# Stick-breaking attention by summation by parts: value differences made at the projection, no weights formed

## The chip, the cores and the metric

One core of one Trainium2 chip runs the whole program. The metric is device time in microseconds (us) of one execution; before, it is 3059.33 us, the median of three runs (3055.2 to 3061.43).

Engines by the profile's names: PE (TensorE matmul) with PEld (its weight loads), DVE (VectorE), ACT (ScalarE), POOL (GpSimd), and SP, whose queue issues all DMAs here. L12 is line 12 of the kernel before.

## What is computed

Two layers run in a row on x of 1024 tokens by 1024 features. Each projects x with `w_in`, runs three token mixers on groups of heads (stick-breaking attention and MLA attention with 4 heads each, RWKV-7 with 8), joins them with `w_o`, normalizes, and ends in a gated FFN with a short convolution. Only the stick-breaking mixer changes:

```python
def stick_breaking_attention(q, k, v):
    ...
        z = jnp.einsum('bhqd,bhkd->bhqk', qb, k).astype(jnp.float32) * scale
        past = kpos[None, :] < qpos[:, None]
        log_keep = jnp.where(past, jax.nn.log_sigmoid(-z), 0.0)
        log_later = lax.cumsum(log_keep, axis=3, reverse=True) - log_keep
        w = jnp.where(past, jnp.exp(jax.nn.log_sigmoid(z) + log_later), 0.0)
        return jnp.einsum('bhqk,bhkd->bhqd', w.astype(v.dtype), v)
```

With keep = sigmoid(-z) and K(j) the product of keep over the positions j and later (1 where masked), the weight is w(j) = K(j+1) - K(j). So the sum of w(j) v(j) is also the sum of K(j) (v(j-1) - v(j)), plus an end term.

## The kernel before

**Phase A** (`phase_a`) works with the transposed activations xTh and xTl in SBUF. Each matrix of weights of 128 columns is loaded and split in a high and a low part (`wload`, L200, L201). Its product with x takes 48 matmuls of 128x512 into the PSUM tile `psmm`, in two halves of 24 (`proj_h`, L205 to L207), and ACT copies each half to a tile `pst` (L253). There are 4 buffers of `pst`, and 3 of `psmm` of one half each.

After the RWKV projections come two recurrent chains of 8 steps (`rw_chain(0)` and `rw_chain(1)`, 4 heads each). Chain 1 needs the result of `rw_inv`, a triangular inverse in small steps on DVE (L725 to L767) and PE (L759, L776, L788), which goes out to DRAM (`psd`, L792) and comes back with each step (`PSl`, L831). A step of a chain is L844 (PE), copies to `QC` (DVE L845, L846, ACT L847), L863 (PE) and L866 (DVE) twice, L871 (PE), and its output `rw_chain_y1`/`y2` (L880 to L906).

`proj_sb` (L263) makes the stick-breaking projections beside this. Its function `step` takes one step of chain 1, whatever number it is given. Before, the order is queries and keys of head pair 0, then of pair 1 (one chain step after each), then the values of both pairs, transposed on PE (L281) and copied on DVE (L282), with one chain step after each pair.

**Attention** follows: MLA (`mla`) and stick-breaking (`stick`) blocks of 128 queries take turns. A stick-breaking block (`stick_block`, `stick_post`) is: scores (PE, L388, L389), tanh (ACT, L390), the mask of the diagonal block (POOL, L396), keep from tanh (DVE, L397), the product scan from the right (DVE, L399), the weight from keep and product (DVE, L400), transposes (PE, L339) with copies to SBUF (ACT, L340), and weights times values (PE, L323) with a scaled copy (ACT, L418). Before, keep and the product sit in one of three tiles that POOL clears first (L1194); they lie in the SBUF of the tiles `LA`, `T` and `pd` of `rw_inv`.

The order on each engine is fixed when the program is built: a scheduler with priorities (`PRIORITY`) and costs of its own sorts the instructions of each engine, and an engine takes them in that order. PSUM and SBUF buffers of one tag go round in the order in which the code asks for them. The transposes of values use the PSUM tags `pa`, `py` and `pq`, which the chains use too.

## Time and profile before

| | |
|---|---|
| median of three runs | 3059.33 us |
| profiled execution, its own time | 3062.54 us |
| its span, first to last instruction | 3060.8 us |
| granted TensorE clock, mean | 0.980 of full speed |
| busy: PE, DVE, ACT, POOL | 96%, 58%, 34%, 8% |

The busy shares are means over stages with different limits. PE is pipelined and the ends of its matmuls are modelled, so a PE at 100% is not at its peak. A row of the windows view gives, for one stretch, the busy us of each engine with its number of instructions, the granted clock, the share of DMA time and the GB/s. Matmuls on plain fp32 data appear as two or more records each.

### The profile page before, as it was taken

The page shows a single profiled execution, that of the slowest core. Times are in us where ns is not written, and L with a number is a line of the kernel's source. Part 1 is how long each engine was busy: PE and PEld are TensorE (multiplying, and loading weights), DVE is VectorE, ACT ScalarE, POOL GpSimd, SP SyncE. Part 2 cuts the span into 40 slices and gives each one's busy share as a digit, 9 for nine tenths or more (in the row PEclk, how much of TensorE's full clock was granted, in tenths as well). Part 3 has the DMA queues.
Part 4 walks back from the last instruction along what each step waited for, and adds up shares of the span by engine and source line. Part 5 has one row for each costly group of instructions (what it writes and reads, how often), then busy time and mean ns, then how long its engine had stood idle before and what let it go on. Part 6 is the DMA issues. An engine that isn't in the chain of part 4 may idle for free.

```text
span 3060.8 us, 41867 instructions
## 1 busy us (share of the span) xinstructions
PE 2941.1 (96%) x16572; PEld 2342.6 (77%) x16572; DVE 1774.8 (58%) x2881; ACT 1045.0 (34%) x1801; POOL 234.2 (8%) x308
## 2 busy tenths in 40 slices
PE   8999999989999999999999999999899999999998
PEld 6766777766888888888877677776678888888887
DVE  4579764886644444444645787658865444444436
ACT  5454443763221112121244543447622111212120
POOL 0001121131000000000000011210300000000000
PEclk9999999899999999999999999999999999999999
DMA  4353656324421111111124446563244111111111
GB/s 132 94 153 107 196 178 202 104 59 138 166 62 56 42 42 49 55 49 56 59 80 112 133 121 202 168 206 93 82 134 165 55 42 42 48 55 49 55 49 55
DMA packets 338259, 301.78 MB, mean 99 GB/s; under 512 B 24200, under 2 KB 302992, under 8 KB 338064
## 3 DMA queue, kind: packets, MB, share of 16 engines
q1 hardware_dynamic: 338064, 299.11, 32.3%
q8 instruction: 131, 2.15, 0.3%
q14 instruction: 64, 0.52, 0.1%
HBM read 208.87 MB, written 90.18 MB: 98 GB/s over the span
## 4 chain that ended last, share of the span: by engine, by line
PE 74%; DVE 11%; issue 8%; ACT 3%; DMA 2%; POOL 1%; SPq 0%; POOLq 0%; DVEq 0%; ACTq 0%
PE psmm L205 16%; PE psmm L206 16%; PE psmm L207 16%; PE psps L205 5%; PE psps L206 5%; PE psps L207 5%; PE pspa L844 1%; DVE pd L729 1%; DVE LA L725 1%; PE pspi L788 1%; PE psmt L216 1%; DVE Aa L767 1%; DVE T L730 1%; PE pspa L684 0%; PE pspy L871 0%
## 5 line engine op out<-in xcount | busy, mean ns | idle before, releaser
L206 PE MATMUL psmm<-xTl,whi 128*128 128x512 f32 x2144 | 851.0, 397 | 0.0
L205 PE MATMUL psmm<-xTh,whi 128*128 128x512 f32 x2144 | 850.4, 397 | 0.0
L207 PE MATMUL psmm<-xTh,wlo 128*128 128x512 f32 x2144 | 848.0, 396 | 0.0
L200 ACT CAST whi<-raw 128x1024 fp32r<-128x1024 f32 x152 | 160.3, 1055 | 1059.5 <-PE psmm L206 1043.0
L205 PEld LDWEIGHTS psmm<-xTh,whi 128*128 128x128 f32 x2144 | 405.1, 189 | 89.0 <-issue 5.4
L207 PEld LDWEIGHTS psmm<-xTh,wlo 128*128 128x128 f32 x2144 | 405.3, 189 | 87.9 <-issue 4.2
L206 PEld LDWEIGHTS psmm<-xTl,whi 128*128 128x128 f32 x2144 | 405.3, 189 | 87.9 <-issue 4.4
L201 DVE TENSOR_TENSOR wlo<-raw,whi 128x1024 fp32r<-128x1024 f32 x152 | 185.5, 1220 | 465.3 <-ACT whi L200 447.9
L1056 DVE TENSOR_TENSOR y<-y,psps 128x512 f32<-128x512 f32 x288 | 196.3, 686 | 171.4 <-PE psps L207 171.3
L205 PE MATMUL psps<-wdh,hh 128*128 128x512 f32 x672 | 266.8, 397 | 0.0
L206 PE MATMUL psps<-wdl,hh 128*128 128x512 f32 x672 | 262.9, 391 | 0.0
L207 PE MATMUL psps<-wdh,hl 128*128 128x512 f32 x672 | 259.7, 391 | 0.0
L205 PEld LDWEIGHTS psps<-wdh,hh 128*128 128x128 f32 x672 | 126.1, 188 | 36.8 <-ACT hh L200 6.0
L919 POOL TENSOR_TENSOR lsm<-lsm,small 128x1 f32<-128x1 f32 x32 | 29.0, 905 | 1634.0 <-DVE lsm L918 1634.0
L207 PEld LDWEIGHTS psps<-wdh,hl 128*128 128x128 f32 x672 | 126.2, 188 | 26.9
L206 PEld LDWEIGHTS psps<-wdl,hh 128*128 128x128 f32 x672 | 126.2, 188 | 25.3
L1031 DVE TENSOR_TENSOR cv<-cv,psmm 128x1024 f32<-128x1024 f32 x44 | 53.7, 1221 | 136.1 <-PE psmm L207 131.1
L201 DVE TENSOR_TENSOR wdl<-raw,wdh 128x1024 fp32r<-128x1024 f32 x42 | 51.5, 1225 | 88.6 <-ACT wdh L200 88.6
L1026 ACT ACTIVATE cv<-cv 128x1024 f32<-128x1024 f32 x44 | 46.8, 1063 | 116.0 <-DVE cv L1025 116.0
L844 PE MATMUL pspa<-RBl,PSl 128*128 128x128 f32 x512 | 73.6, 291 | 11.9 <-ACT QC L847 8.9
L844 PEld LDWEIGHTS pspa<-RBl,PSl 128*128 128x128 f32 x512 | 66.5, 200 | 19.5 <-ACT QC L847 10.8
L206 PE MATMUL psmm<-wol,whi 128*128 128x512 f32 x192 | 76.9, 401 | 2.0 <-DVE wol L201 2.0
(442 smaller groups left out, 4568.2 us busy)
## 6 DMA issues: line engine op xcount, KB each, us to landing
raw<-in_ffn_w_up_dram SPq DMA_DIRECT2D x88, 512.0 KB
raw<-in_w_in_dram SPq DMA_DIRECT2D x44, 512.0 KB
raw<-in_ffn_w_down_dram SPq DMA_DIRECT2D x44, 512.0 KB
rbd<-RB SPq DMA_DIRECT2D x64, 256.0 KB
PSl<-psd SPq DMA_DIRECT2D x32, 512.0 KB
RBl<-rbd SPq DMA_DIRECT2D x32, 512.0 KB
psd<-Vz SPq DMA_DIRECT2D x64, 128.0 KB
xxd<-X SPq DMA_DIRECT2D x64, 128.0 KB
```

The lines of the kernel that those rows point to most:

```text
L200: self.nc.scalar.copy(hi, src)
L201: (eng or self.nc.vector).tensor_tensor(lo, src, hi.bitcast(F32), op=ALU.subtract)
L205: mm(out, lh, rh, start=start, stop=False)
L206: mm(out, lh, rl, start=False, stop=False)
L207: mm(out, ll, rh, start=False, stop=stop)
L216: nc.tensor.transpose(pt[:, k * P : k * P + P], xt[:, kk * P : kk * P + P], self.ident)
L725: nc.vector.transpose(LA[r], Af[r, :, q // 2, x0 : x0 + 32].rearrange("p f t -> p t f"))
L729: mul = lambda o, x, y: nc.vector.tensor_tensor(o, x, y, op=ALU.mult)
L844: nc.tensor.matmul(pQ[:, f, e, :], PSh[:, f, h, e, :], RBh[:, f, h, e, :], start=True, stop=True)
L1026: nc.scalar.activation(cv, cv, AF.Gelu)
L1031: nc.vector.tensor_tensor(cv, cv, pg, op=ALU.mult)
L1056: nc.vector.tensor_tensor(y[:, i, hs], y[:, i, hs], ps, op=ALU.add)
```

## The change

1. `proj_sb` projects the values first. From the projected values `d` it makes differences `e` on DVE (e[t] = d[t-1] - d[t], e[0] = -d[0]), transposes and stores them in `svd[0]`; then it replaces the last column of each block of 128 by d[t-1] (the end term), transposes again and stores that in `svd[1]`. So each pair of heads now has two sets of transposes, copies and stores, and one chain step after each set.
2. Queries and keys follow, with one chain step after each, as before. All 8 steps of chain 1 are now asked for inside `proj_sb`; before it was 6.
3. `stick_post` forms keep in place, scans in place, and transposes the scan's result. The weight (L400) is gone, and so are the three cleared tiles.
4. `attn_out` takes the end-term values for the last block and the plain differences for the others. The scale of 0.5 in `av_store` becomes a plain copy.
5. The difference values are loaded into the tiles `LA` and `T` (pair 0), and `pd` and a new tile `mdd` (pair 1).

```diff
     def proj_sb(self, l, pool, step):
         nc, W = self.nc, self.a["w_in"][l]
         for j in range(2):
+            hi, lo = self.wload(W, [(SBV + j * P, P)])
+            d = self.t(pool, [P, S], "pst", bufs=4)
+            self.proj_copy(hi, lo, d)
+            e = self.t(pool, [P, S], "pst", bufs=4)
+            nc.vector.tensor_tensor(e[:, 1:S], d[:, 0 : S - 1], d[:, 1:S], op=ALU.subtract)
+            nc.vector.tensor_scalar(e[:, 0:1], d[:, 0:1], -1.0, None, op0=ALU.mult)
+            self.store_v(e, self.svd[0, j], pool)
+            step(2)
+            nc.vector.tensor_copy(e[:, P - 1 : S : P], d[:, P - 2 : S : P])
+            self.store_v(e, self.svd[1, j], pool)
+            step(2)
+        for j in range(2):
             for base, dst in ((SBQ, self.sqd), (SBK, self.skd)):
...
                 step(4)
-        for j in range(2):
-            hi, lo = self.wload(W, [(SBV + j * P, P)])
...
-            nc.sync.dma_start(self.svd[j], o.rearrange("p (i v) -> p i v", v=P))
+
+    def store_v(self, e, dst, pool):
+        nc = self.nc
+        o = self.t(pool, [P, S], "pst", bufs=4)
+        for q in range(2):
+            pt = self.ps2()
+            for i in range(4):
+                ii = 4 * q + i
+                nc.tensor.transpose(pt[:, i * P : i * P + P], e[:, ii * P : ii * P + P], self.ident)
+            nc.vector.tensor_copy(o[:, q * 512 : q * 512 + 512], pt)
+        nc.sync.dma_start(dst, o.rearrange("p (i v) -> p i v", v=P))
...
-                ms.append(self.nc.tensor.matmul(av[hc], V[:, j, hc], wts[hp][:, j, :], start=j == 0, stop=j == nb - 1))
+                ms.append(self.nc.tensor.matmul(av[hc], (Vd if j == nb - 1 else V)[:, j, hc], wts[hp][:, j, :], start=j == 0, stop=j == nb - 1))
...
+    def stick_steps(self, wp, pr):
+        r3 = lambda t: t.rearrange("p (j v) -> p j v", v=P)
+        if pr:
+            V = r3(self.t(self.ip, [P, S], "pd")), self.t(wp, [P, NT, P], "mdd", bufs=1)
+        else:
+            V = tuple(r3(self.t(self.ip, [P, S], n)) for n in ("LA", "T"))
+        for u in range(2):
+            self.nc.sync.dma_start(V[u], self.svd[u, pr])
+        return V
...
-        nc.vector.tensor_scalar(kp[:, : LL - 1], be[:, 1:LL], -0.5, 0.5, op0=ALU.mult, op1=ALU.add)
-        kv = kp[:, : LL - 1][:, ::-1]
-        nc.vector.tensor_tensor_scan(kv, kv, self.ones.to_broadcast([P, LL - 1]), 1.0, op0=ALU.mult, op1=ALU.mult)
-        nc.vector.scalar_tensor_tensor(be[:, :LL], be[:, :LL], 1.0, kp[:, :LL], op0=ALU.add, op1=ALU.mult)
+        nc.vector.tensor_scalar(be[:, :LL], be[:, :LL], -0.5, 0.5, op0=ALU.mult, op1=ALU.add)
+        kv = be[:, :LL][:, ::-1]
+        nc.vector.tensor_tensor_scan(kv, kv, self.ones.to_broadcast([P, LL]), 1.0, op0=ALU.mult, op1=ALU.mult)
...
-        nc.scalar.mul(ot, av, sc)
+        nc.scalar.copy(ot, av)
```

The scheduler sorts anew, and three places move. In the rows below the lines of the changed kernel are its own: its L292 and L293 are the transposes and copies of `store_v`, L294 its store, L370 the load of difference values; L792, L804, L805 and L808 are L776, L788, L789 and L792 of before, and L847, L850, L860, L863, L879 and L896 are L831, L834, L844, L847, L863 and L880 of before. L205 to L207 and L253 are the same lines in both.

**PE, first layer, at the start of chain 1.** Before, this stands there (`psmm` is a projection, `pspa<-RBl,PSl` the first work of a chain step):

```order
L206 MATMUL psmm_4538<-xTl_133,whi_4506 128x512
L207 MATMUL psmm_4538<-xTh_132,wlo_4507 128x512
L205 MATMUL psmm_4538<-xTh_132,whi_4506 128x512
L844 MATMUL pspa_4067<-RBl_4058,PSl_4059 128x128 x4
L844 MATMUL pspa_4075<-RBl_4058,PSl_4059 128x128 x4
L206 MATMUL psmm_4538<-xTl_133,whi_4506 128x512
L207 MATMUL psmm_4538<-xTh_132,wlo_4507 128x512
L205 MATMUL psmm_4538<-xTh_132,whi_4506 128x512
L844 MATMUL pspa_4113<-RBl_4104,PSl_4105 128x128 x4
L844 MATMUL pspa_4121<-RBl_4104,PSl_4105 128x128 x4
L863 MATMUL pspy_4083<-S_514_3175,QC_4066 64x64 x4
```

Now it is this, from the last work of `rw_inv` on (`pspi<-T`), `pspa<-ident,pst` being a transpose of values:

```order
L804 MATMUL pspi_3898<-LA_3896,Aa_878 128x128 x4
L804 MATMUL pspi_3904<-LA_3896,Aa_878 128x128 x4
L804 MATMUL pspi_3956<-T_3954,Aa_878 128x128 x4
L804 MATMUL pspi_3962<-T_3954,Aa_878 128x128 x4
L860 MATMUL pspa_4083<-RBl_4074,PSl_4075 128x128 x4
L860 MATMUL pspa_4091<-RBl_4074,PSl_4075 128x128 x4
L860 MATMUL pspa_4129<-RBl_4120,PSl_4121 128x128 x4
L879 MATMUL pspy_4099<-S_514_3175,QC_4082 64x64
L860 MATMUL pspa_4137<-RBl_4120,PSl_4121 128x128 x4
L879 MATMUL pspy_4099<-S_514_3175,QC_4082 64x64 x3
L292 MATMUL pspa_4161<-ident_65,pst_4055 128x128 x4
```

Before, 112 projection matmuls of `proj_sb` stand between the first L759 of the second `rw_inv` and the first L844 of chain 1, and 59 behind that. Now 0 stand there and 168 behind, the first of them 56 rows after the chain's start. In the second layer it was 112 and 59 too, and is now 48 and 120, the first one 88 rows after the chain's start. Behind the last projection the chain work of before (16 and 24 matmuls of L863 in the two layers) is gone.

**ACT, first layer, the same place.** Before (`LA<-pspi` and `T<-pspi` end `rw_inv`, `QC` is a chain step, `pst<-psmm` releases a projection):

```order
L789 COPY LA_3896<-pspi_3898 128x512
L789 COPY LA_3896<-pspi_3904 128x512
L789 COPY T_3954<-pspi_3956 128x512
L789 COPY T_3954<-pspi_3962 128x512
L200 CAST whi_4646<-raw_4645 128x1024
L253 COPY pst_4384<-psmm_4411 128x512
L253 COPY pst_4511<-psmm_4512 128x512
L847 COPY QC_4066<-pspa_4067 64x2x256
L847 COPY QC_4066<-pspa_4075 64x2x256
L847 COPY QC_4112<-pspa_4113 64x2x256
L847 COPY QC_4112<-pspa_4121 64x2x256
L253 COPY pst_4511<-psmm_4538 128x512
```

Now:

```order
L805 COPY T_3954<-pspi_3956 128x512
L805 COPY T_3954<-pspi_3962 128x512
L863 COPY QC_4082<-pspa_4083 64x2x256
L863 COPY QC_4082<-pspa_4091 64x2x256
L863 COPY QC_4128<-pspa_4129 64x2x256
L863 COPY QC_4128<-pspa_4137 64x2x256
L896 COPY ys_4147<-pspy_4099 128x256
L897 ACTIVATE yq_4145<-ys_4147 128x256
L863 COPY QC_4197<-pspa_4198 64x2x256
L863 COPY QC_4197<-pspa_4206 64x2x256
L253 COPY pst_4228<-psmm_4229 128x512
L253 COPY pst_4228<-psmm_4255 128x512
```

The two copies at the end are those of the second pair's values. They are what frees `psmm` for the next projections, and they now stand behind the first two steps of chain 1 (three pairs of `QC`) and the first step's output.

**SP, first layer, in chain 1.** Before, the store of values stands behind the loads of a chain step, and its load comes in the attention phase:

```order
L831 DMA PSl_4807<-psd_122 128x1024
L832 DMA RBl_4806<-rbd_120 128x1024
L833 DMA arl_4808<-ard_123 128x256
L284 DMA svd_117<-pst_4564 128x1024
L530 DMA mv_4939<-mvd_116 128x1024
L533 DMA pst_4941<-mqd_114 96x1024
```

Now (`svd<-pst` is a store of value differences, `LA`, `T` and `pd<-svd` load them):

```order
L849 DMA arl_4403<-ard_123 128x256
L294 DMA svd_117<-pst_4154 128x1024
L370 DMA T_5203<-svd_117 128x1024
L847 DMA PSl_4529<-psd_122 128x1024
L848 DMA RBl_4528<-rbd_120 128x1024
L849 DMA arl_4530<-ard_123 128x256
L294 DMA svd_117<-pst_4284 128x1024
L294 DMA svd_117<-pst_4366 128x1024
L370 DMA pd_6317<-svd_117 128x1024
L850 DMA bvl_4404<-bvd_124 128x256
```

The loads of `T` and `pd` now stand one and two rows behind stores that they read from, in front of `PSl` loads of chain 1.

## Rows read from the trace of the kernel before

**Rows 1.** The page's parts 1 and 4: busy time, and the chain that ended last.

```profile
PE 2941.1 (96%) x16572; PEld 2342.6 (77%) x16572; DVE 1774.8 (58%) x2881; ACT 1045.0 (34%) x1801; POOL 234.2 (8%) x308
...
PE 74%; DVE 11%; issue 8%; ACT 3%; DMA 2%; POOL 1%; SPq 0%; POOLq 0%; DVEq 0%; ACTq 0%
```

**Rows 2.** Windows of the first layer: rw_inv's end, chain 1, after the projections, attention.

```profile
core 0: us, PE busy (x) PEld busy (x) DVE busy (x) ACT busy (x) POOL busy (x), PEclk, DMA share, GB/s
414.20:475.70 61.50, 58.17 (x589) 48.20 (x588) 24.91 (x47) 23.89 (x46) 15.35 (x16) 0.94 0.56 164
475.70:518.70 43.00, 42.92 (x367) 33.88 (x368) 22.75 (x67) 14.53 (x30) 7.02 (x8) 1.00 0.58 193
518.70:545.00 26.30, 21.33 (x167) 17.86 (x166) 19.31 (x52) 16.23 (x35) 5.50 (x7) 0.87 0.67 185
545.00:722.00 177.00, 154.95 (x1144) 116.44 (x1143) 150.37 (x292) 119.19 (x302) 37.04 (x50) 0.93 0.31 91
```

**Rows 3.** Windows of the second layer, the same four stretches.

```profile
1939.60:2000.30 60.70, 58.29 (x589) 48.17 (x588) 24.88 (x47) 23.90 (x46) 15.33 (x16) 0.94 0.56 164
2000.30:2038.90 38.60, 38.59 (x338) 32.00 (x339) 20.86 (x61) 13.77 (x29) 6.69 (x7) 1.00 0.65 222
2038.90:2066.50 27.60, 22.75 (x203) 18.84 (x201) 20.96 (x58) 17.02 (x38) 6.14 (x8) 0.94 0.66 184
2066.50:2242.00 175.50, 152.48 (x1142) 114.17 (x1141) 149.42 (x291) 118.51 (x300) 35.94 (x50) 0.95 0.31 92
```

**Rows 4.** Windows of L400 alone, in the attention stretches of both layers.

```profile
core 0: us, DVE busy (x), PEclk, DMA share, GB/s
545.00:722.00 177.00, 25.07 (x32) 0.93 0.31 91
2066.50:2242.00 175.50, 25.15 (x32) 0.95 0.31 92
```

**Rows 5.** Windows inside the first layer's attention, and one of chain steps without projections.

```profile
520.00:535.00 15.00, 10.91 (x102) 8.83 (x100) 11.43 (x26) 9.88 (x17) 1.96 (x3) 1.00 0.88 253
555.00:575.00 20.00, 17.36 (x89) 12.88 (x89) 15.01 (x40) 11.56 (x33) 2.64 (x5) 0.66 0.46 138
585.00:595.00 10.00, 10.00 (x85) 7.74 (x84) 9.81 (x23) 9.40 (x24) 0.13 (x2) 1.00 0.12 32
580.00:620.00 40.00, 37.22 (x325) 29.65 (x325) 38.57 (x81) 32.23 (x85) 2.17 (x5) 1.00 0.26 67
```

**Rows 6.** Waits of PE in the first layer's attention (us in total, times, longest).

```profile
PE psav L339 <- DVE mexp L580: 5.0, 5, 2.7
PE psmm L205 <- ACT whi L200: 3.2, 1, 3.2
PE pspa L339 <- DVE mst L566: 2.6, 2, 2.4
...
PE pspa L339 <- DVE mexp L400: 1.9, 4, 0.8
```

**Rows 7.** Timeline of PE, second layer: a run of 39 projection matmuls, its ends.

```profile
1991.23 0.40 PE L206 MATMUL psmm<-xTl,whi 128*128 128x512 f32 x1
...
1999.89 0.39 PE L205 MATMUL psmm<-xTh,whi 128*128 128x512 f32 x1
```

**Rows 8.** The chain of waits, first layer, from rw_inv's last matmul to chain 1.

```profile
464.74 0.97 PE pspi L788 x8
...
465.73 0.60 ACT T L789
...
466.97 3.99 DMA psd<-T
...
471.03 4.71 DMA PSl<-psd
...
475.78 1.27 PE pspa L844 x9
```

**Rows 9.** Timeline of PE, first layer: four transposes of values and what follows.

```profile
500.61 0.66 PE L281 MATMUL pspa<-ident,pst 128*128 128x128 f32 x4
501.20 0.33 PE L863 MATMUL pspy<-S,QC 128*64 128x64 f32 x2
```

**Rows 10.** DVE groups: a copy of transposed values; an elementwise operation of 128x1024.

```profile
L282 DVE COPY pst<-pspa 128x512 f32<-128x512 f32 x2 | 1.4, 690 | 0.0
...
L201 DVE TENSOR_TENSOR wlo<-raw,whi 128x1024 fp32r<-128x1024 f32 x152 | 185.5, 1220 | 465.3 <-ACT whi L200 447.9
```

**Rows 11.** Timeline of PE, first layer: the same eight records at two clocks.

```profile
442.83 1.78 PE L788 MATMUL pspi<-LA,Aa 128*128 128x128 f32 x8
...
445.64 1.06 PE L788 MATMUL pspi<-LA,Aa 128*128 128x128 f32 x8
```

More of the change, by code (lines that the diff above doesn't have):

```diff
@@ L76, in __init__ @@
         self.sq = 0
-        self.sn = self.kn = 0
+        self.sn = 0
         self.pairs = {}
@@ L271, in proj_sb @@
                 step(4)
-        for j in range(2):
-            hi, lo = self.wload(W, [(SBV + j * P, P)])
-            d = self.t(pool, [P, S], "pst", bufs=4)
-            self.proj_copy(hi, lo, d)
-            o = self.t(pool, [P, S], "pst", bufs=4)
-            for q in range(2):
-                pt = self.ps2()
-                for i in range(4):
-                    ii = 4 * q + i
-                    nc.tensor.transpose(pt[:, i * P : i * P + P], d[:, ii * P : ii * P + P], self.ident)
-                nc.vector.tensor_copy(o[:, q * 512 : q * 512 + 512], pt)
-            step(4)
-            nc.sync.dma_start(self.svd[j], o.rearrange("p (i v) -> p i v", v=P))
+    def store_v(self, e, dst, pool):
[8 more added lines that the diff above has]
+        nc.sync.dma_start(dst, o.rearrange("p (i v) -> p i v", v=P))
     def proj_mla(self, l, pool):
@@ L390, in stick_block, with stick_post @@
             nc.scalar.activation(be[:, a0:a1], s, AF.Tanh, scale=0.0625)
[L391 to L393 removed]
+        self.stick_post(be, i, LL, nb, n, V, hp, pr, wp)
+    def stick_post(self, be, i, LL, nb, n, V, hp, pr, wp):
         nc = self.nc
@@ L584, in mla_post @@
         wt = self.w_transpose(self.wt4[:, self.sn % 6], e, nb)
-        self.pair(("m", pr, i), wt, hp, nb, V, self.mixd[2 + pr], i, wp, "av", 1.0)
+        self.pair(("m", pr, i), wt, hp, nb, V, V, self.mixd[2 + pr], i, wp, "av")
     def q2(self, tp):
@@ L1191, in run @@
                 self.wt4 = self.t(self.ip, [P, 6, NT, P], "Aa")
-                self.kp3 = [self.t(self.ip, [P, S], n) for n in ("LA", "T", "pd")]
-                for t in self.kp3:
-                    nc.gpsimd.memset(t, 0.0)
                 for t in range(MLA_AHEAD):
```

17 lines of the change are left out of this document (6 added, 11 removed).

## Prediction

> **What bounds the kernel now.** I read the page first. PE is busy for 96% of the span, and the chain that ended last is PE for 74% and DVE for 11% [rows 1]. So an operation taken off DVE is worth something only where PE waits for DVE, and an instruction added to PE costs its whole time where PE has no gap. The windows show where that is. Each layer has four stretches that the change touches [rows 2, 3]: the end of `rw_inv` (PE busy 58.17 of 61.5 us in the first layer, 58.29 of 60.7 in the second), chain 1 with projections beside it (42.92 of 43.0 and 38.59 of 38.6: no gap), the rest of chain 1 without projections (21.33 of 26.3 and 22.75 of 27.6), and attention (154.95 of 177.0 and 152.48 of 175.5). PE idles for 22.0 and 23.0 us in attention, and for 5.0 and 4.85 us behind the last projection. It idles little in the other two stretches because projection matmuls lie between the small steps of `rw_inv` and of chain 1. The change lowers the work of DVE in attention, and it moves these projections.
>
> **The work removed.** L400 was 32 instructions per layer, 25.07 and 25.15 us of DVE [rows 4], in stretches where DVE is busy for 150.37 and 149.42 us [rows 2, 3]. The memsets of three tiles were on POOL, which is 8% busy [rows 1], and cost nothing. A copy with a scale and a plain copy are the same pass of ACT over the same tile: nothing.
>
> How much of the 25 us comes back? PE cannot gain more than it idles, 22 us, except by the clock: in 555 to 575 the granted clock is 0.66 (a mix of the levels 2.4 and 1.2 GHz) [rows 5], and fewer waits for DVE may keep it up there. By rows, 20 us at 0.66 lose 20 x 0.34 = 6.8 us. The upper bound is then 22 + 7 = 29 us per layer. The lower bound is 0: in 580 to 620, where DVE is fullest (38.57 of 40 us), PE is busy for 37.22 us already, and in 585 to 595 both are full (10.00 and 9.81 of 10) [rows 5]. The waits of PE that name DVE are also partly of other kinds: MLA's copies and maxima (L566, L580) stand above those for L400 [rows 6], and the former remain. They do come sooner when DVE has a sixth less to do (25 of 150). I take two thirds of the idle time, 15 us, and 2 for the clock: **-17 us per layer**.
>
> **The work added.** There are 16 more transposes on PE per layer. Four of them take 500.61 to 501.20, 0.59 us [rows 9]; so 4 x 0.59 = **+2.4 us per layer**, because they stand among projections where PE has no gap. DVE gets four more copies of 0.69 us and two subtractions of about 1.22 us [rows 10], with the two small column operations some 5.5 us. In chain 1 DVE is busy for 22.75 of 43 us [rows 2], so PE's projections hide them. One subtraction of the first pair can stand ahead of the last DVE steps of `rw_inv`, which chain 1 waits for: **+1.2 us per layer** (0 if it is late, 2.4 if both are). If that cover went, all 5.5 us would be exposed. On SP two more stores and two more loads are issued. The loads of `T` and `pd` stand right behind the stores that they read, so SP waits until a store has landed. A store of this size took 3.99 us to land [rows 8]. Queued behind the wait are `PSl` loads of later steps of chain 1. Chain 1 would then be late by up to 4 us twice, while 168 projections x 0.228 us = 38 us (below) are there for PE to do: I price it at nothing, and at 8 us per layer at most if they are used up.
>
> **The work moved.** This is the largest term. Projection matmuls follow each other every (1999.89 - 1991.23) / 38 = 0.228 us [rows 7]. In the first layer 112 of them leave the stretch of `rw_inv`: 112 x 0.228 = 25.5 us of PE work. In the second layer it is 112 - 48 = 64, or 14.6 us. What remains there is a chain of latencies: from the last L788 at 464.74 through a copy of 0.60 us, a store of 3.99 and a load of 4.71 to the first L844 at 475.78, none of which the absence of projections shortens [rows 8]. So that stretch stays about as long, PE idles in it, and the same work comes behind the start of chain 1, where PE was full: **+25.5 and +14.6 us**. The upper bound is these figures; below, the stretch may shrink, because small PE steps no longer stand behind a projection matmul. With some 20 such groups in series, and 0.228 us in front of each, that gives 4.6 us.
>
> Behind the chain's start 56 and 88 rows of PE come ahead of the first projection, since `psmm` is released only by ACT copies behind two steps of chain 1. How full is PE in steps without projections? In 520 to 535 it is busy for 10.91 of 15 us [rows 5], 27% idle. Over some 15 us of such steps that is **+4 us per layer** (0 to 6).
>
> What is regained: projections now last until chain 1 ends, and fill the gaps of 5.0 and 4.85 us behind the last projection [rows 2, 3]: **-5.0 and -4.85 us**.
>
> **The clock.** In the first 62 us the mean granted clock is 0.94 [rows 2], although projections keep PE nearly full. The same eight records of L788 took 1.78 us once and 1.06 us another time [rows 11], so PE's small steps can be longer by 0.72 us per group at the low level. Eight such groups in series are 5.8 us. The sum takes nothing for this, since most groups there ran at the short time; a rival does. The Trainium skill, "TensorE: Matmul & The Clock Gate", Part 1, says that the throttled clock is the default and that activity releases it. By that rule an emptied stretch would run at the low level and the sum would be higher by these 5.8 us per layer or more; here the trace agrees in so far as the lowest clock, 0.66, falls in a window where PE was busy for 17.36 of 20 us [rows 5].
>
> **The sum.** First layer: 25.5 + 2.4 + 4 + 1.2 - 5.0 - 17 = +11.1 us. Second: 14.6 + 2.4 + 4 + 1.2 - 4.85 - 17 = +0.35 us. Together +11.4 us on the profiled execution, 3062.54 us, which gives 3074.0. That execution stands 3.2 us above the median of 3059.33, so the median to expect is 3070.8, rounded 3071 us. About 0.2%, 6.1 us, is what a measurement of this kernel can tell from no change.
>
> **The rivals.**
>
> A, the forecast: the lost cover of `rw_inv` outweighs what DVE's relief gives to attention. For it speak the two full windows of [rows 2, 3] and the counts of the order; against it, that the upper bound of attention's gain (29 us) is above the work moved (25.5 us). Its terms vary by about 8 us below and 9 above: 3055 to 3080. Chance 0.43.
>
> B, faster: PE in attention waits above all for DVE, and gets 26 us per layer back, while the gap at the chain's start is 2 us. First layer: 25.5 + 2.4 + 2 + 1.2 - 5.0 - 26 = +0.1; second: 14.6 + 2.4 + 2 + 1.2 - 4.85 - 26 = -10.65. That gives 3062.5 - 10.5 - 3.2 = 3049 us, and 3040 if the emptied stretch also shrinks by 4.6 us in each layer. It decides once attention gains over 17 + 11.4 / 2 = 22.7 us per layer. For it: 25 us are removed from an engine that is busy for 85% of these stretches. Against it: the full windows at 585 to 595 [rows 5]. Chance 0.36.
>
> C, slower by much: the emptied stretch runs at the low clock, so its serial path grows by eight groups x 0.72 = 5.8 us [rows 11] and some 2 us in its other matmuls (8 us in the first layer, 6 in the second, where 48 projections remain), and attention gains only 10 us per layer, since PE is the bound wherever DVE is full. That adds 14 + 2 x 7 = 28 us: 3071 + 28 = 3099 us. It decides where the granted clock of the stretch falls well below the 0.94 of now. For it: the 0.66 beside DVE waits [rows 5]. Against it: the clock stood at 1.00 in 520 to 535 with PE 27% idle, in the same rows. Chance 0.21.
>
> That the change doesn't do what it says needs no case: no weight is left in the order of DVE.
>
> **How the numbers follow.** The likeliest case gives 3071 us. The range reaches from the better end of B to nearly all of C: 3038 to 3096 us, with about 2 in 10 outside. B gives most of faster (0.33). The lower third of A and a little of B lie within 0.2% (0.19). The rest of A and all of C are slower (0.48).
>
> **What would show it.** PE busy 15 to 25 us below the 58.17 of now between `rw_inv`'s first L759 and chain 1; a gap of projections at the chain's start; the last projection some 35 us later than 518.7 in the first layer, with no idle time behind it; attention at about 160 us in place of 177, with DVE busy for about 125; SP waiting some 4 us at the loads of `T` and `pd` with PE busy meanwhile. I am wrong if attention shrinks by over 22.7 us, if the stretch before chain 1 shortens by much or other PE work fills it, or if the granted clock there falls below 0.9.

## The result, and the profile after

The changed kernel took 3125.07 us (median of 4 runs, 3124.58 to 3127.08), before 3057.26 us (4 runs). The ratio is 1.022, 95% interval 1.0207 to 1.0233: slower by 68 us. The forecast was 3071 us, +11.4. The sign was right, but the size lies outside the range, whose end was 3096.

| | after |
|---|---|
| profiled execution, its own time | 3125.13 us |
| its span | 3123.4 us |
| granted TensorE clock, mean | 0.970 |
| busy: PE, DVE, ACT, POOL | 95%, 56%, 33%, 7% |

The page's part 1, which answers to [rows 1]:

```profile
PE 2964.5 (95%) x16604; PEld 2356.8 (75%) x16604; DVE 1745.8 (56%) x2837; ACT 1040.3 (33%) x1801; POOL 232.7 (7%) x302
```

DVE has 29 us less to do (50 are gone with L400, and the rest takes 21 more, of which the prediction had 11), and PE has 32 instructions and 23 us more. The 32 transposes explain 5 of the 23 us. The number of the others is unchanged, so they took longer; where, the windows show by the granted clock.

Windows of the changed kernel, first layer, cut where its own work changes: from the second `rw_inv`'s first matmul to chain 1, from there to the last projection, on to the first scan of stick-breaking, and to the last scan. The columns are those of [rows 2].

```profile
417.98:482.70 64.72, 38.13 (x449) 32.02 (x450) 21.89 (x41) 17.82 (x36) 11.27 (x12) 0.68 0.52 150
482.70:576.20 93.50, 90.30 (x600) 67.48 (x601) 36.97 (x100) 25.69 (x51) 11.91 (x12) 0.98 0.45 146
576.20:609.49 33.29, 25.74 (x105) 19.18 (x104) 20.80 (x50) 20.42 (x46) 4.20 (x5) 0.58 0.59 168
609.49:751.13 141.64, 126.30 (x1059) 99.01 (x1057) 113.99 (x232) 105.56 (x273) 33.84 (x47) 0.98 0.27 79
```

The same for the second layer:

```profile
1978.49:2041.18 62.69, 46.65 (x501) 38.98 (x501) 25.80 (x45) 19.74 (x39) 11.27 (x12) 0.82 0.53 156
2041.18:2120.40 79.22, 75.46 (x548) 57.54 (x549) 34.49 (x96) 23.47 (x48) 11.01 (x12) 0.97 0.51 172
2120.40:2153.14 32.74, 25.50 (x108) 19.24 (x106) 20.89 (x51) 20.42 (x46) 4.19 (x5) 0.58 0.60 169
2153.14:2293.34 140.20, 124.77 (x1058) 97.70 (x1055) 114.33 (x233) 105.84 (x273) 33.02 (x47) 0.99 0.28 80
```

And the kernel before, cut at the same events: chain 1's start to the first scan and first to last scan, in the first and then in the second layer, and, last, from the last projection of the first layer to its first scan.

```profile
475.78:561.92 86.14, 79.41 (x629) 62.70 (x629) 55.11 (x154) 44.82 (x101) 15.36 (x17) 0.95 0.62 190
561.92:711.00 149.08, 132.45 (x1022) 101.06 (x1021) 133.24 (x254) 102.68 (x260) 34.22 (x47) 0.94 0.25 73
2000.31:2082.28 81.97, 75.03 (x629) 60.46 (x629) 54.16 (x153) 43.61 (x101) 14.39 (x17) 0.98 0.66 207
2082.28:2229.50 147.22, 129.89 (x1020) 98.85 (x1020) 132.99 (x253) 103.23 (x260) 34.37 (x47) 0.97 0.24 72
518.88:561.92 43.04, 36.31 (x262) 28.66 (x260) 32.36 (x87) 30.29 (x71) 8.15 (x10) 0.90 0.66 189
```

Three readings. **The emptied stretch** did not shorten. It was 61.5 us [rows 2] and is 64.72; PE is busy for 38.13 us, and the granted clock is 0.68. **Chain 1's start to the first scan** grew from 86.14 to 93.50 + 33.29 = 126.79 us, and in the second layer from 81.97 to 79.22 + 32.74 = 111.96: +40.7 and +30.0 us. Within it, from the last projection to the first scan, the granted clock is 0.58, where it was 0.90. **Between the scans** the time fell by 7.4 and 7.0 us. DVE's work fell by 19 us there, but PE's idle time only from 16.6 to 15.3 us and from 17.3 to 15.4. The other 6.1 and 5.1 us are PE busy time, at a granted clock of 0.98 and 0.99 in place of 0.94 and 0.97.

Together that is 3.2 + 40.7 - 7.4 in the first layer and 2.0 + 30.0 - 7.0 in the second, 61.5 us of the 62.6 by which the spans differ. The cut at the first scan is a convenience: matmuls of attention that aren't done before it come behind it, and the changed kernel has 37 and 38 more records of PE between its scans (1059 and 1058, where it was 1022 and 1020).

The low clock is seen in single instructions. First the end of `rw_inv` in the timeline of PE (L804 is L788 of before, L860 is L844):

```profile
462.06 2.05 PE L804 MATMUL pspi<-LA,Aa 128*128 128x128 f32 x8 [5.25 <-DMA LA<-xxd]
464.78 2.08 PE L804 MATMUL pspi<-LA,Aa 128*128 128x128 f32 x8 [0.67 <-ACT LA L805]
467.53 2.08 PE L804 MATMUL pspi<-T,Aa 128*128 128x128 f32 x8 [0.68 <-ACT LA L805]
470.33 2.07 PE L804 MATMUL pspi<-T,Aa 128*128 128x128 f32 x8 [0.72 <-ACT T L805]
482.70 4.71 PE L860 MATMUL pspa<-RBl,PSl 128*128 128x128 f32 x24 [10.29 <-DMA PSl<-psd]
```

Eight records take 2.07 us, where they took 0.97 [rows 8]. What was hidden behind projections now stands open: 5.25 us for a load, 0.7 us for each copy of ACT, 10.29 us for the store and load of `psd`. Then three scores of MLA at the start of attention, after:

```profile
596.13 0.69 PE L205 MATMUL pssc<-kh,qh 96*128 96x384 f32 x1 [0.18 <-ACT mexp L583]
596.62 0.52 PE L206 MATMUL pssc<-kl,qh 96*128 96x384 f32 x1
596.94 0.52 PE L207 MATMUL pssc<-kh,ql 96*128 96x384 f32 x1
```

and before:

```profile
554.36 0.42 PE L205 MATMUL pssc<-kh,qh 96*128 96x384 f32 x1
554.62 0.34 PE L206 MATMUL pssc<-kl,qh 96*128 96x384 f32 x1
554.80 0.34 PE L207 MATMUL pssc<-kh,ql 96*128 96x384 f32 x1
```

### The profile page after: what moved, and what is told of

Its sections match the earlier page's. It is cut to its first block, busy times and chain, and to the rows that moved or that the text cites. A ratio compares the mean times of both kernels' runs of the same rounds, so it can differ in the third digit from the quotient of the medians.

```text
span 3123.4 us, 41922 instructions
## 1 busy us (share of the span) xinstructions
PE 2964.5 (95%) x16604; PEld 2356.8 (75%) x16604; DVE 1745.8 (56%) x2837; ACT 1040.3 (33%) x1801; POOL 232.7 (7%) x302
## 5 line engine op out<-in xcount | busy, mean ns | idle before, releaser
L205 PE MATMUL psmm<-xTh,whi 128*128 128x512 f32 x2144 | 852.7, 398 | 1.7 <-ACT pst L253 1.6
L207 PE MATMUL psmm<-xTh,wlo 128*128 128x512 f32 x2144 | 848.9, 396 | 0.0
L205 PEld LDWEIGHTS psmm<-xTh,whi 128*128 128x128 f32 x2144 | 405.0, 189 | 92.1 <-issue 5.4
L207 PEld LDWEIGHTS psmm<-xTh,wlo 128*128 128x128 f32 x2144 | 404.9, 189 | 88.1 <-issue 4.2
L205 PE MATMUL psps<-wdh,hh 128*128 128x512 f32 x672 | 266.7, 397 | 0.0
L207 PE MATMUL psps<-wdh,hl 128*128 128x512 f32 x672 | 259.6, 391 | 0.0
L205 PEld LDWEIGHTS psps<-wdh,hh 128*128 128x128 f32 x672 | 126.1, 188 | 36.7 <-ACT hh L200 5.9
L207 PEld LDWEIGHTS psps<-wdh,hl 128*128 128x128 f32 x672 | 126.2, 188 | 26.9
L206 PEld LDWEIGHTS psps<-wdl,hh 128*128 128x128 f32 x672 | 126.2, 188 | 25.5
L860 PE MATMUL pspa<-RBl,PSl 128*128 128x128 f32 x512 | 78.6, 306 | 28.0 <-DMA PSl<-psd 15.5
L860 PEld LDWEIGHTS pspa<-RBl,PSl 128*128 128x128 f32 x512 | 70.8, 214 | 37.3 <-ACT QC L863 13.9
L416 DVE TENSOR_TENSOR_SCAN mexp<-mexp,small 128x128 f32<-128x128 f32 (+7 forms) x64 | 88.0, 1378 | 0.8
```

What stands on the lines that cost most here:

```text
L205: mm(out, lh, rh, start=start, stop=False)
L206: mm(out, lh, rl, start=False, stop=False)
L207: mm(out, ll, rh, start=False, stop=stop)
L416: nc.vector.tensor_tensor_scan(kv, kv, self.ones.to_broadcast([P, LL]), 1.0, op0=ALU.mult, op1=ALU.mult)
L860: nc.tensor.matmul(pQ[:, f, e, :], PSh[:, f, h, e, :], RBh[:, f, h, e, :], start=True, stop=True)
```

## The experiments

All ratios are to the kernel before, run on the same chip. The runs were made in four groups, in which the median of the kernel before lay between 3056.17 and 3058.49 us, so a difference between runs of two groups is good to some 2 us.

Three theories go through the expectations. Theory 1: the loss comes from projections that left the stretch of `rw_inv`. Theory 2: with the arithmetic in place, a tile is held too long, and that takes back what DVE's relief gives. Theory 3: a second loss stands beside that of theory 1, because the end of chain 1 no longer lies beside the start of attention, which it covered.

| run | what it is | us | ratio, 95% interval |
|---|---|---|---|
| e2 | before, values first | 3080.20 | 1.0075 (1.0062 to 1.0088) |
| e19 | e2 with 8 steps | 3114.58 | 1.0189 (1.0173 to 1.0205) |
| e5 | changed, one set | 3107.31 | 1.0158 (1.0145 to 1.0171) |
| e3b | changed, transposes in `psmm` | 3093.47 | 1.0118 (1.0100 to 1.0136) |
| e10 | changed, 6 steps | 3097.35 | 1.0131 (1.0109 to 1.0152) |
| e10b | changed, 4 steps | 3084.48 | 1.0090 (1.0068 to 1.0112) |
| e14 | e3b and 6 steps | 3076.05 | 1.0061 (1.0047 to 1.0075) |
| e4 | before without L400 | 3035.56 | 0.9935 (0.9921 to 0.9949) |
| e6 | before, arithmetic in place, one set | 3043.73 | 0.9948 (0.9935 to 0.9960) |
| e1 | changed, queries and keys first | 3058.30 | 1.0004 (0.9996 to 1.0013) |
| e11 | e1 with 6 steps | 3056.38 | 1.0004 (0.9990 to 1.0017) |
| e7 | e1, product in own tiles | 3056.25 | 0.9998 (0.9989 to 1.0006) |
| e9 | e7, one set and end rows | 3048.85 | 0.9972 (0.9958 to 0.9985) |
| e12 | e9 with 6 steps | 3044.27 | 0.9953 (0.9936 to 0.9970) |
| e17 | e9 with 4 steps | 3069.05 | 1.0036 (1.0024 to 1.0049) |

Three of them leave something out: e5 the end term, and e4 and e6 multiply the products by plain values.

### From before to the changed kernel, one part at a time

**e2: values first, in the old arithmetic.** The two loops of `proj_sb` change places.

```diff
     def proj_sb(self, l, pool, step):
         nc, W = self.nc, self.a["w_in"][l]
+        for j in range(2):
+            hi, lo = self.wload(W, [(SBV + j * P, P)])
...
         for j in range(2):
             for base, dst in ((SBQ, self.sqd), (SBK, self.skd)):
...
-        for j in range(2):
-            hi, lo = self.wload(W, [(SBV + j * P, P)])
...
```

> The kernel before with only the order of the projections changed: values first, then queries and keys; weights formed as before, one set of transposes. 51 and 81 projection matmuls stay in the stretch of rw_inv in the two layers (112 and 112 before). Theory 1: 92 matmuls move behind the start of chain 1, at 0.23 to 0.45 us each: 3078 to 3098 us. Rival (the order alone is harmless, the second set and the differences are what hurts): 3053 to 3062 us.

It took 3080.2 us: theory 1, 23 us for 92 moved matmuls, 0.25 us each. The spacing in [rows 7] is 0.228.

**e19: the same with 8 steps of chain 1 asked for.**

```diff
                 nc.vector.tensor_copy(o[:, q * 512 : q * 512 + 512], pt)
             step(4)
+            step(4)
```

> The kernel before with values first, as in e2_values_first_old, and with 8 steps of chain 1 asked for inside proj_sb in place of 6: the old arithmetic and one set. 120 matmuls stand behind the chain's start in both layers (e2: 120 and 90), and no matmul of the chain behind the first score of MLA (e2: 44). Theory 3 (the end of the chain beside the start of attention is worth some 13 us per layer): 30 x 0.25 = 8 us for the matmuls and 20 to 28 for the two layers' cover: 3106 to 3118 us. Rival (the cover is worth little; what six steps gave in the changed kernel were its 48 matmuls in the first layer): 3084 to 3092 us.

It took 3114.58 us, 34.4 more than e2: theory 3. Windows of the first layer from the last projection to the first scan and on to the last scan, e2:

```profile
540.62:580.40 39.78, 33.67 (x258) 26.42 (x257) 30.60 (x88) 29.37 (x71) 6.78 (x9) 0.96 0.64 173
580.40:723.18 142.78, 127.08 (x1017) 96.38 (x1015) 130.47 (x251) 103.36 (x260) 34.84 (x47) 0.98 0.27 76
```

and e19:

```profile
551.92:580.52 28.60, 21.04 (x84) 15.30 (x82) 17.50 (x42) 16.59 (x38) 4.19 (x5) 0.59 0.59 165
580.52:736.35 155.83, 137.00 (x1086) 105.59 (x1085) 140.58 (x272) 110.94 (x282) 32.88 (x47) 0.95 0.27 81
```

In e2 PE has 258 matmuls in the start of attention, since the end of chain 1 lies beside it, at a granted clock of 0.96. In e19 the chain is done before the last projection, 84 matmuls are left, and the clock is 0.59. e19 has less of attention done when its first scan starts, and needs 13 us more from there to the last. Both reach their first scan at the same time (580.40 and 580.52 us), so the whole loss of this layer shows behind it. The stretch of `rw_inv` is no different (61.46 and 61.42 us).

**e5: the changed kernel without its second set.**

```diff
-            nc.vector.tensor_copy(e[:, P - 1 : S : P], d[:, P - 2 : S : P])
-            self.store_v(e, self.svd[1, j], pool)
-            step(2)
...
-            self.nc.sync.dma_start(V[u], self.svd[u, pr])
+            self.nc.sync.dma_start(V[u], self.svd[0, pr])
```

> The changed kernel without the second set (no column replaced, no second transposes, copies and stores; the plain differences are loaded twice, so the end term of the last block is left out). 48 projection matmuls stand in the stretch of rw_inv in each layer (changed kernel 0 and 48, before 112 and 112). Theory 1 (the loss goes with the matmuls that leave this stretch; values first in the old arithmetic lost 23 us for 92 of them): 128 of them at 0.25 to 0.39 us: 3085 to 3105 us. Rival (the second set's own transposes, stores and waiting loads cost most of the 68 us): 3060 to 3078 us.

It took 3107.31 us, just above the range of theory 1. Its rival is out, although the second set does cost 17.8 us (3125.07 - 3107.31), more than its transposes: without it 48 projections stay in the first layer's stretch of `rw_inv` in place of none. From e19 to e5 only the arithmetic changes (with the differences and the tiles that the values are loaded into), in kernels with 120 matmuls behind the chain's start and no chain work behind the first score. It gains 7.3 us.

The four steps make a chain: values first +23.0 (e2), two more steps +34.4 (e19), the arithmetic -7.3 (e5), the second set +17.8. Together +67.9 us, which is the whole loss. The shares hold for this sequence of steps; in other kernels below the same parts are worth something else.

### Repairs with values first

**e3b: the transposes of values in the projections' PSUM.**

```diff
     def store_v(self, e, dst, pool):
...
-            pt = self.ps2()
+            pt = self.mm_ps()
```

> The changed kernel, values still first, but their transposes go to the PSUM tag of the projections in place of the three tags of the chains. 97 projection matmuls stand in the stretch of rw_inv in each layer (0 and 48 in the changed kernel). Theory 1, with the cause that the transposes wait for PSUM that the chains hold and so block the ring of tiles: about 146 matmuls return, 33 us of PE work and most of the idle time: 3070 to 3090 us. Rival (queries and keys that are projected last come late for attention, wherever the rest stands): above 3105 us.

It took 3093.47 us, 3 us above the range, with 31.6 us regained. The windows of `rw_inv`'s end and of the start of attention in the first layer:

```profile
418.22:473.90 55.68, 48.71 (x544) 40.29 (x544) 26.68 (x46) 19.31 (x38) 10.77 (x11) 1.00 0.66 204
549.10:581.64 32.54, 25.29 (x108) 19.09 (x106) 20.79 (x51) 20.42 (x46) 4.21 (x5) 0.58 0.60 170
```

The edit touches nothing but the PSUM of the transposes, so it was this choice of PSUM that held the projections back. That the transposes wait there for the chains, that it goes by way of the ring `pst`, whose tiles come free late, and of ACT's copies, which then release `psmm` late, is read from the order and not shown apart. With 97 projections in the stretch it takes 55.68 us at a clock of 1.00, in place of 64.72 at 0.68. The start of attention is as uncovered as in the changed kernel, 0.58.

**e10 and e10b: 6 and 4 steps asked for.**

```diff
             self.store_v(e, self.svd[0, j], pool)
-            step(2)
             nc.vector.tensor_copy(e[:, P - 1 : S : P], d[:, P - 2 : S : P])
             self.store_v(e, self.svd[1, j], pool)
             step(2)
```

e10b also drops the last line.

> The changed kernel, values first and both sets, but with 6 steps of chain 1 asked for inside proj_sb, as before, in place of 8 (none after a pair's first set). 120 projection matmuls stand behind chain 1's start in each layer (changed kernel 168 and 120, before 59 and 59), and 44 matmuls of the chain stand behind the first score of MLA (changed kernel 0, before 24). Theory 3 (two losses: 0.25 us for each matmul that leaves the stretch of rw_inv, and some 13 us per layer because the chain's end no longer stands beside the start of attention): 122 x 0.25 = 30 us, less 8 to 14 us that the arithmetic gains: 3072 to 3086 us. Rival (only the moved projections count; the one-set kernel with the same 120 took 3107 us): 3100 to 3115 us.

> As e10_six_steps, but with 4 steps asked for, none among the values. 104 and 105 projection matmuls stand behind chain 1's start, 92 matmuls of the chain behind the first score of MLA. Theory 3: 91 x 0.25 = 23 us, less the arithmetic's gain: 3065 to 3080 us, 5 to 10 below e10_six_steps. Rival (the chain that is left over makes oproj late, which needs its output): 5 us or more above e10_six_steps.

They took 3097.35 and 3084.48 us. Both miss their ranges, 11 and 4 us above. The direction holds: 28 us come back with 6 steps, and 13 more with 4. These 28 us aren't the cover's alone, since with 6 steps 48 projections also stay in the first layer's stretch of `rw_inv`, in place of none. For e10 the end of `rw_inv` and the start of attention read:

```profile
417.56:480.16 62.60, 47.98 (x510) 39.67 (x510) 26.30 (x47) 19.80 (x39) 11.26 (x12) 0.82 0.57 166
545.68:584.50 38.82, 32.94 (x256) 26.04 (x255) 30.83 (x87) 29.49 (x71) 6.78 (x9) 0.95 0.60 165
```

The start of attention is mended (0.95), while the stretch of `rw_inv` still idles for 14.6 us. Theory 3 took its price per moved matmul from e2, and a gain of the arithmetic of 8 to 14 us; which of them is too favourable here, and so what the 11 us are, was not settled.

**e14: both repairs.**

```diff
-            pt = self.ps2()
+            pt = self.mm_ps()
...
             self.store_v(e, self.svd[0, j], pool)
-            step(2)
```

> The changed kernel with both repairs, values still first: transposes of values in the projections' PSUM (as e3b_transposes_mm, 3093 us) and 6 steps asked for (as e10_six_steps, 3097 us). 97 matmuls stay in the stretch of rw_inv, 143 stand behind chain 1's start, 44 matmuls of the chain behind the first score of MLA. Theory 3: the cover is a loss of its own and comes off e3b's time too: 3064 to 3076 us. Rival (both repairs mend the same loss): 3085 to 3095 us.

It took 3076.05 us, at the upper end of theory 3's range. 6 steps take 17.4 us off e3b's time, so the uncovered start is a loss of its own. Its worth per layer is 8.7 us here, and (34.4 - 7.5) / 2 = 13.5 from e2 to e19, where 7.5 is 30 matmuls at 0.25. Windows from chain 1's start to the first scan, in both layers, for e3b:

```profile
473.90:581.64 107.74, 99.17 (x658) 76.30 (x658) 53.34 (x142) 43.25 (x93) 15.21 (x17) 0.87 0.52 161
2012.72:2121.09 108.37, 99.37 (x658) 76.24 (x658) 52.91 (x142) 42.94 (x92) 15.19 (x17) 0.87 0.51 159
```

and for e14:

```profile
478.13:581.69 103.56, 97.78 (x698) 74.90 (x699) 53.84 (x155) 46.63 (x105) 14.32 (x17) 0.98 0.55 170
2003.12:2107.03 103.91, 98.34 (x698) 75.57 (x699) 54.44 (x154) 47.13 (x107) 14.39 (x17) 0.97 0.56 170
```

With the cover this stretch is 4.2 and 4.5 us shorter, though 40 more records of PE lie in it. The scans behind it take 2.6 us less in each layer (137.41 and 137.64 in place of 140.03 and 140.18).

### The arithmetic

**e4: before without L400.**

```diff
-        nc.vector.scalar_tensor_tensor(be[:, :LL], be[:, :LL], 1.0, kp[:, :LL], op0=ALU.add, op1=ALU.mult)
-        wt = self.w_transpose(self.wt4[:, n % 6], be, nb, "pa")
+        wt = self.w_transpose(self.wt4[:, n % 6], kp, nb, "pa")
```

> The kernel before with L400 alone left out: the product is transposed in place of the weight (so the stick-breaking output is the sum of products times values), with everything else in its order. This is the gain that taking the operation off DVE has by itself. The prediction took 17 us per layer: 3023 us. What the changed kernel shows between the first and the last scan of attention, 7 us per layer: 3043 us. Rival (DVE is hidden there anyway): 3053 to 3061 us.

It took 3035.56 us, 21.7 us less, or 11 per layer: between the 17 of the prediction and the 7 between the scans. From the first to the last scan, in the first and in the second layer:

```profile
558.99:700.16 141.17, 124.28 (x1017) 97.41 (x1017) 112.68 (x224) 101.75 (x260) 33.65 (x47) 0.96 0.28 76
2064.90:2203.74 138.84, 122.56 (x1016) 96.22 (x1017) 112.00 (x223) 102.40 (x261) 33.06 (x47) 0.98 0.27 76
```

That is 7.9 and 8.4 us less than before, but PE idles as long as it did: 16.9 and 16.3 us, before 16.6 and 17.3. What fell is its busy time, by 8.2 and 7.3 us for nearly the same number of matmuls.

**e1: the changed kernel, queries and keys first.** The two loops of the changed `proj_sb` change places.

```diff
+        for j in range(2):
+            for base, dst in ((SBQ, self.sqd), (SBK, self.skd)):
...
         for j in range(2):
             hi, lo = self.wload(W, [(SBV + j * P, P)])
...
-        for j in range(2):
-            for base, dst in ((SBQ, self.sqd), (SBK, self.skd)):
...
```

> The changed kernel with only the order of the projections undone: queries and keys first, then the values with their differences and both sets of transposes. 112 projection matmuls stand again between the second rw_inv's first L759 and chain 1 in both layers. Theory 1 (the loss comes from projections that left the stretch of rw_inv): the loss is gone and only the arithmetic is left, which gains some 7 us per layer in attention and costs 2 to 4 us per layer in added transposes and copies: 3042 to 3055 us. Rival (the new arithmetic itself, with its second set of transposes, stores and waits on SP, costs the time): above 3100 us.

It took 3058.3 us. The rival is out: put back in order, the loss is gone. But the gain isn't there either: it is 3 us above theory 1's range. That led to theory 2, in the next runs. The trace shows where it is missing. To the first scan e1 takes about as long as the kernel before (85.35 and 83.20 us from chain 1's start; before 86.14 and 81.97), and between the scans it gains nothing:

```profile
560.40:709.47 149.07, 132.23 (x1084) 102.84 (x1083) 118.96 (x240) 108.24 (x281) 34.16 (x47) 0.97 0.29 81
2078.45:2228.04 149.59, 132.52 (x1084) 103.26 (x1083) 118.97 (x239) 108.37 (x281) 34.42 (x47) 0.96 0.28 81
```

e1 has 62 and 64 more records of PE there than the kernel before, since with 8 steps asked for less of attention is done when the first scan starts.

**e6: before, with the arithmetic in place and one plain set.**

```diff
-        nc.vector.tensor_scalar(kp[:, : LL - 1], be[:, 1:LL], -0.5, 0.5, op0=ALU.mult, op1=ALU.add)
+        nc.vector.tensor_scalar(be[:, :LL], be[:, :LL], -0.5, 0.5, op0=ALU.mult, op1=ALU.add)
...
-        nc.vector.scalar_tensor_tensor(be[:, :LL], be[:, :LL], 1.0, kp[:, :LL], op0=ALU.add, op1=ALU.mult)
```

> The kernel before with its projections as they were (one plain set of values), and the changed kernel's arithmetic of a block: keep in place, scan in place, the scan's result transposed, no L400, no cleared tiles (the sum of products times plain values). Theory 2 (in place, the product holds the tile mexp from tanh until its transposes, and the three tiles that took keep and product before are gone, so the relief of DVE is given back as waits for mexp): 3048 to 3060 us. Rival (the arithmetic gains 22 us here as with L400 alone left out, and the added work of phase A is what ate it in the kernel with queries and keys first): 3030 to 3040 us.

It took 3043.73 us, 14.8 us less than the kernel before beside it (3058.49). That lies between the two ranges, some 4 us from either, and decides nothing by itself. It is not clearly apart from e4 either, as the two intervals overlap.

**e7: e1 with a ring of three tiles for keep and product.**

```diff
-        nc.vector.tensor_scalar(be[:, :LL], be[:, :LL], -0.5, 0.5, op0=ALU.mult, op1=ALU.add)
-        kv = be[:, :LL][:, ::-1]
+        kp = self.t(wp, [P, S], "kp", bufs=3)
+        nc.vector.tensor_scalar(kp[:, :LL], be[:, :LL], -0.5, 0.5, op0=ALU.mult, op1=ALU.add)
+        kv = kp[:, :LL][:, ::-1]
```

> Queries and keys first as in e1_qk_first, with both sets of transposes, but keep and product go to a ring of three tiles of their own in place of mexp. Theory 2 (tiles held too long): most of the 22 us come back, less 2 to 4 us per layer of added work: 3038 to 3048 us. Rival (the added work of phase A ate the gain): 3053 to 3061 us, as e1_qk_first.

3056.25 us, 2 us from e1 and within the rival's range: theory 2 fails for the whole time. Between the scans the tiles of their own do help, 144.95 and 145.06 us in place of e1's 149.07 and 149.59, but from the last scan to the end e7 takes 835.5 us, e1 830.0. That the gain is lost in phase A, as the rival says, e7 doesn't show: up to the first scan it takes 85.30 and 83.72 us, about as long as the kernel before.

**e11: e1 with 6 steps.**

```diff
             self.store_v(e, self.svd[0, j], pool)
-            step(2)
```

> Queries and keys first as in e1_qk_first, both sets, with 6 steps of chain 1 asked for inside proj_sb in place of 8. 28 and 24 matmuls of the chain stand behind the first score of MLA (24 and 24 before, 0 in e1_qk_first). Theory 3: the 14.6 us between e1_qk_first and e6_in_place were the lost cover of attention's start: 3041 to 3048 us. Rival (they are the second set's transposes, copies and stores): 3054 to 3060 us.

3056.38 us, within 2 us of e1: theory 3 misses here, and the time is in the rival's range. With queries and keys first, the two steps are worth 2 us in place of 17 or 34. So the 12.7 us between e11 and e6 (3056.38 - 3043.73) are not the number of steps. What else differs is the second set, the differences, and the tiles that the values are loaded into. Their cost lies ahead of the first scan. From chain 1's start to there, in both layers, e6:

```profile
476.49:562.35 85.86, 77.94 (x630) 61.33 (x630) 55.60 (x154) 44.50 (x101) 14.65 (x17) 0.98 0.64 196
1993.72:2074.72 81.00, 73.72 (x631) 59.44 (x632) 54.61 (x159) 44.34 (x102) 14.45 (x17) 1.00 0.66 208
```

and e11:

```profile
471.64:561.67 90.03, 79.72 (x646) 64.52 (x646) 60.70 (x163) 44.19 (x101) 15.66 (x17) 0.94 0.67 211
1995.26:2085.69 90.43, 79.36 (x646) 64.60 (x646) 61.73 (x165) 44.04 (x101) 17.90 (x17) 0.94 0.67 208
```

That is 4.2 and 9.4 us more; between the scans it is 1.7 and 1.1 (146.32 and 135.74 against 144.60 and 134.68).

### A faster kernel

**e9: e7 with one transposed set.** The eight columns that differ are transposed alone and written over the last row of the second tile.

```diff
-            nc.vector.tensor_copy(e[:, P - 1 : S : P], d[:, P - 2 : S : P])
-            self.store_v(e, self.svd[1, j], pool)
+            pt = self.ps2()
+            x8 = self.t(pool, [P, S], "pst", bufs=4)
+            nc.vector.tensor_copy(x8[:, :NT], d[:, P - 2 : S : P])
+            nc.tensor.transpose(pt[:NT, :P], x8[:, :NT], self.ident)
+            nc.vector.tensor_copy(x8[:NT, P : 2 * P], pt[:NT, :P])
+            nc.sync.dma_start(self.sed[j], x8[:NT, P : 2 * P])
...
-            self.nc.sync.dma_start(V[u], self.svd[u, pr])
+            self.nc.sync.dma_start(V[u], self.svd[0, pr])
+        self.nc.sync.dma_start(V[1][P - 1 : P], self.sed[pr : pr + 1])
```

> As e7_own_tiles, but the differences are transposed once; the eight end columns alone are transposed by one small transpose and written over the last row of the second loaded tile. Per layer 14 transposes and two stores of 512 KB are gone. If the added work of phase A costs what the prediction took (2.4 us per layer on PE and no time for the rest): 5 us below e7_own_tiles. Rival (it stands beside other work): the same as e7_own_tiles within 3 us. If theory 2 holds too, this is the fastest of the correct kernels: 3032 to 3044 us.

3048.85 us, above its range. It is 7.4 us below e7, somewhat more than the transposes' own time.

**e12 and e17: e9 with fewer steps.** e12 drops the first line marked, e17 both. Since this is done for either pair, e17 asks for 4 steps, not for 5 as its expectation says; the 24 matmuls counted there are those of the kernel that ran.

```diff
             self.store_v(e, self.svd[0, j], pool)
-            step(2)
...
             nc.sync.dma_start(self.sed[j], x8[:NT, P : 2 * P])
-            step(2)
```

> As e9_end_rows (one set and end rows, product in its own tiles), with 6 steps of chain 1 asked for. Theory 3: the cover comes back here too, 8 to 15 us below e9_end_rows: 3033 to 3041 us. Rival (12 matmuls of the chain behind the first score are too few, or the second set was the cost and is gone already): 3046 to 3051 us.

> As e12_end_rows_six, but with 5 steps asked for (none after the second pair's values): 24 matmuls of the chain stand behind the first score of MLA in place of 12. Theory 3: as much cover as before, 3 to 8 us below e12_end_rows_six: 3036 to 3042 us. Rival (the cover that counts is there already): 3042 to 3047 us.

e12 took 3044.27 us, 0.9953 of before (0.9936 to 0.9970): the fastest of those that compute the whole reference, though 3 us above the expected range. e17 took 3069.05 us, 25 more than e12, which neither theory had. In the first layer the windows from the last projection to the first scan and to the last scan are, for e12:

```profile
510.85:559.47 48.62, 37.80 (x297) 30.03 (x297) 35.15 (x100) 30.56 (x73) 9.78 (x10) 0.89 0.58 180
559.47:693.60 134.13, 120.80 (x1005) 95.60 (x1004) 106.89 (x214) 96.36 (x254) 36.21 (x47) 0.96 0.26 73
```

and for e17:

```profile
513.95:568.12 54.17, 42.37 (x313) 33.87 (x312) 37.96 (x102) 31.75 (x76) 11.91 (x11) 0.91 0.60 179
568.12:709.57 141.45, 125.63 (x1001) 98.01 (x1001) 108.63 (x218) 97.09 (x253) 32.74 (x47) 0.93 0.23 66
```

The clock of the start is no lower in e17 (0.91), yet both stretches are longer, with PE idle for 11.8 and 15.8 us in place of 10.8 and 13.3. More of the chain behind the last projection is thus no gain by itself. What holds it up was not followed further.

## Why the prediction was wrong

**The forecast's mechanism, projections that leave the stretch of `rw_inv`, is there.** PE's idle time in it grew from 3.3 to 26.6 us and from 2.4 to 16.0; the terms were 25.5 and 14.6 us. e2 gives 0.25 us per moved matmul against the 0.228 assumed. In e1, where they stay, the loss is gone.

**"What is regained", -5.0 and -4.85 us, failed, and this is the largest miss.** From chain 1's start to the first scan the prediction had +28.1 us in the first layer and +17.35 in the second (its terms without attention); measured were +40.7 and +30.0, 12.6 us more in each. The stretch behind the last projection was read as 5 us of waste that projections would fill. But PE's 21.33 us of work there [rows 2] were the end of the chain and the start of attention side by side. When projections last longer than the chain, attention starts alone, on scores and exponentials that wait for each other. From 576.20 to 609.49 PE idles for 7.5 us, and the granted clock is 0.58. The two more steps, of which the prediction says nothing, made this so: e19 shows 34.4 us for them in the old arithmetic, e14 17.4 us the other way. Both have values first; with queries and keys first they are worth 2 us (e1 against e11), so it takes the late projections too. Not all of the 12.6 us is this term. As an estimate, about 9 are: the 5 that were to be regained, and the 4.2 and 4.5 by which e3b is longer than e14 up to the first scan. The rest is the higher price of a moved matmul (22 ns for 112 and 64 of them, 2.5 and 1.4 us) and the added work below. And part of what the lost cover costs lies behind the first scan, where e19 shows all of its 13 us.

**The clock, taken as nothing in the sum, fell where rival C had it fall.** The emptied stretch ran at 0.68 and 0.82, in place of 0.94 [rows 2, 3]. It got 3.2 and 2.0 us longer, less than C's 8 and 6, although a group of eight records took 1.1 us more (2.07 against 0.97), where C had 0.72. C did not see the second place, the start of attention. Its own figure was 3099 us, already beyond the end of the range at 3096, and 26 us short of the result. The Trainium skill, "TensorE: Matmul & The Clock Gate", Part 1, has the throttled clock as the default that activity releases. For the emptied stretch the rows agree, with 0.68 and PE busy for 38.13 of 64.72 us. The start of attention is not as clear a case: its clock is 0.58 while PE is busy for 25.74 of 33.29 us.

**Attention's -17 us was too large, and what it was made of was not what came.** Between the scans it was -7.4 and -7.0; with L400 alone taken out, 21.7 us of the whole time, or 11 per layer; in place, 14.8, or 7.4 per layer. DVE fell from 133.24 to 113.99 us between the scans, and PE's idle time by 1.3 us only. The term was 15 us of PE's idle time, as if that were waiting for DVE's throughput, and 2 for the clock. The idle time did not come back even where L400 alone is gone (e4: 33.2 us in both layers, before 34.0); PE's busy time fell instead, by 15.5 us. By busy time and granted clock (0.96 and 0.98 in place of 0.94 and 0.97) some 4 us of these are the clock, as an estimate; what the rest is stays open. The full windows of [rows 5], which set the lower bound, were nearer.

**The added work, 2.4 + 1.2 us per layer, was too small.** With queries and keys first and 6 steps, the changed kernel is 12.7 us slower than its arithmetic in place with one plain set (e11 against e6), 6.3 per layer, with 4.2 and 9.4 us of it ahead of the first scan; one set and end rows take 7.4 us off in all (e9 against e7).

**Right were:** the largest term and its place, the 4 us of idle time at the chain's start (3.2 and 3.8 us from there to the last projection), and no cost of SP's waits. The wait for a store at L370 was there, shorter than the 3.99 us taken for each, in the waits of SP's queue from 410 to 620 us:

```profile
SPq L370 <- DMA svd<-pst: 5.1, 2, 2.7
```

PE was busy for 90.30 of 93.50 us meanwhile.

In sum, per layer 12.6 us from chain 1's start to the first scan, about 10 between the scans and 2 to 3 in the emptied stretch were missed, 50 us in all.

## What to carry to other kernels

Idle time between two phases need not be a gap to be filled: look at which work of both phases lies side by side there, and ask whether the moved work ends before or after the one that covers the next phase's start. When a loop is put in another order, follow the PSUM that its transposes use, because it can decide which independent work still runs beside a latency chain: here that choice alone was worth 31.6 us. An operation that is taken off an engine which is not the bound gives back less than its busy time (here 14.8 and 21.7 of 50 us), and the idle time of the bound does not tell how much: between the scans it stayed the same here. A second set of values, with its differences, transposes, copies and stores, took 12.7 us back.

## What was unexpected of the hardware

PE's records can be nearly gapless at half clock: from 595.00 to 609.50 us of the changed kernel PE was busy for 14.32 of 14.50 us with scores, transposes and short products, at a granted clock of 0.50:

```profile
595.00:609.50 14.50, 14.32 (x56) 10.67 (x56) 9.92 (x26) 9.80 (x23) 0.29 (x1) 0.50 0.55 159
```

So a busy share near 1 did not mean here that PE worked at its full rate. With the chain's end beside the same scores, as in e10, the clock of that start was 0.95.
